# The first half of each pair's combination, with its loads, four turns sooner

## The chip, the core and the metric

The kernel runs on one core of a Trainium2 chip. The metric is the device time of one execution in microseconds (us). The core has five engines that work beside each other: PE (TensorE: matmuls and transposes), DVE (VectorE), ACT (ScalarE), POOL (GpSimd) and SP, which here only issues transfers (DMAs). Each engine does its own instructions in the order in which they are written into the program, and waits where an operand isn't ready. "PEld" in the profile is PE's loading of weights, which overlaps its matmuls.

## The reference

One layer of a decoder over 2048 tokens of width 1024, all in 32-bit floating point: a norm and one combined input projection, two mixers side by side, an output projection, a squared-ReLU MLP and a last norm. Mixer A is gated linear attention (GLA) in chunks, a recurrence over the tokens. Mixer B is dilated attention with 8 heads of 64 in three branches, which are then combined:

```
outs, lses = [], []
for window, dilation in ((128, 1), (512, 4), (2048, 16)):
    o, lse = dilated_branch(q, k, v, rel_bias, window, dilation)
    outs.append(o)
    lses.append(lse)
w = jax.nn.softmax(jnp.stack(lses, axis=0), axis=0)
return jnp.sum(w[..., None] * jnp.stack(outs, axis=0), axis=0)
...
mixed = jnp.concatenate([o_a, o_b], axis=-1)
h = h + jnp.einsum('bsm,md->bsd', mixed, w_out)
```

The last `sum` is the combination: for each token and head, the three branches' outputs are weighted by their softmax denominators and added.

## The kernel before

The program has stages one behind the other: the norm with the input projection (to about 522 us), the attention stage (to about 885 us), the output projection with the second norm, the MLP and the last norm. The change touches the attention stage alone.

**Turns.** The stage takes the 8 heads as four pairs (`pr` 0 to 3). Each head of a pair runs its branch 2 (dilation 16), then 1, then 0. A branch is cut into units of two or four blocks of 128 queries: 4 units for branch 2, 8 for branch 1, 8 for branch 0, so 40 units a pair and 160 in all. The main loop takes one turn for each unit. In a turn it writes, interleaved, the score matmuls of the unit three ahead (`AHEAD`; PE L764 and L766 into the PSUM banks `ps_c`, then DVE L776 adds the bias and takes the minimum, and ACT L777 the exponential, both in `pe`), the transposes of the present unit (PE L786 into `ps_d`, copied to `pt` by ACT L793 or DVE L795), and the products with the values of the unit two back (PE L805 into `ps_a`; DVE L808 copies the sums to the branch's output `O`). There are 384 score operations on DVE, two or four in a unit; places in the order are counted in them.

**GLA.** Beside the turns a generator gives one step of the GLA's 16 chunks at a time, 56 steps in 100 turns. A chunk is a chain over the engines: PE L932, ACT L933 and L934, POOL L935, L938 and L940, PE L945, DVE L946, PE L965 and L966, ACT L967 and L969, POOL L982, ACT L984, PE L990, DVE L993. All of PE's results in it go through one bank, `ps_o`. `gv` and `sr` are loaded by SP at L924 and L925. A chunk's 16 matmuls at L965 and L966 need its four at L945.

**The combination.** Branches 1 and 2 of a pair go to DRAM (`boD`) in their own order of tokens, and come back in the order of branch 0. While pair `pr` runs, pair `pr - 1` is combined, in two halves of 1024 tokens. Each half has two loads (SP L830, `cmb<-boD`) and eight steps, one a turn. Half 0 has its weights in the tile `small`; half 1 has them in a part of a GLA tile, which the profile names `gla`. The steps are: the minimum of the three logarithms' parts (DVE L842, L843) and its differences (POOL L845); the exponential (ACT L848) and the sum of the denominators (POOL L849 to L852); the reciprocal (DVE L855) and the weights (POOL L857); then, for each four tokens' tiles, the three multiplications and two additions (POOL L863 and L865). At the end a store of the combined tokens to `mixD` is noted, which SP issues three turns later (L882). Pair 3's own combination follows at the stage's end in four quarters and goes partly to DVE; the change leaves it alone.

**Other work on the same engines.** POOL also packs the queries for the dilated branches (L718, `qp<-qs`). In the last 28 turns `load_wo` brings in W_out in eight chunks: a load by SP (L1005, `woraw<-w_out`), a rounding on ACT (L1006) and the remainder on DVE (L1007).

**What sets the order.** The turns give what is written when. A scheduler then places each engine's instructions, by its own simulation of the times, so that one engine's instructions may stand in another order than the loop's. The minimum L842, the exponential L848 and the reciprocal L855 are held in program order (`tc.keep_in_program_order`). All tiles in SBUF called by `slot` share one ring of 25 places.

Of the kernel before, what the change touches and what calls it, by code (L numbers as in the profile page):

```python
# [38 lines left out]
def emit(tc, a, stop=99):  # L39
# [459 lines left out]
    def load_head(h):  # L499


        pr, hh = divmod(h, 2)
        t = pairs[h] = [slot("qs", FR, S)]
        pin(SP.dma_start(t[0].bitcast(F32), qD[pr][64 * hh:64 * hh + 64].rearrange("r d s -> (r d) s")), h)
        yield
        for part in range(2):
            t.append(slot(f"k{part + 1}", FR, S))
            rows = kD[pr][64 * hh:64 * hh + 64, part]
            pin(SP.dma_start(t[-1].bitcast(F32), bass.AP(tensor=rows.tensor, offset=rows.offset,
                                                         ap=[[2 * S, 64], [0, 2], [1, S]])), h)  # L510
            yield
# [313 lines left out]
    def combine_load(pr, half):  # L825

        ts, u = slice(8 * half, 8 * half + 8), slot("cmb")
        R = [view(u[:, 1056 * b:], (8, 132)) for b in range(2)]
        for b in range(2):
            SP.dma_start(R[b], boD[pr][b].rearrange("(t p) n -> p t n", p=128)[:, ts])  # L830
        return R
# [212 lines left out]
    def at_unit(n, *f):  # L1044
        plan.setdefault(n, []).append(f)
# [3 lines left out]
    def combine_at(pr, t0, n, at, steps):  # L1049

        if at is not None:
            at_unit(at + AHEAD, lambda: got.update({(pr, t0 // 8): combine_load(pr, t0 // 8)}))

        def step():
            if (pr, t0) not in running:
                running[pr, t0] = combine(pr, t0, n, got[pr, t0 // 8], V if pr == 3 and t0 % 8 else G)
            next(running[pr, t0], None)

        for k in steps:
            at_unit(k + AHEAD, step)  # L1060

    for pr in range(4):
        seq = [(hh, br) for hh in range(2) for br in (2, 1, 0)]
        if pr == 3:
            seq = [(0, 2), (0, 1), (1, 2), (1, 1), (0, 0), (1, 0)]
        for hh, br in seq:
            b = Branch()
            b.h, b.br = 2 * pr + hh, br
            m = 4 if br == 2 else 2
            first = len(units)  # L1070
            if br:
                for part in range(4) if first else ():
                    at_unit(first - 4 + part, pack_q, b.h, br, part)
            if br == 2 and first:
                pieces = load_head(b.h)
                for n in (13, 11, 8):
                    at_unit(first - n, lambda p: next(p), pieces)
                if hh == 0:
                    for half in range(2):
                        combine_at(pr - 1, 8 * half, 8, first - 2 + 7 * half, [first + 4 + 7 * half + n for n in range(8)])  # L1080
            if (pr, br) != (3, 0):
                for n in range(0, NT, m):
                    units.append(Unit(b, range(n, n + m)))
            elif hh:
                for n in range(0, NT, 4):
                    for w in (was, b):
                        units.extend(Unit(w, range(n + k, n + k + 2)) for k in (0, 2))
                for n, at in ((0, 8), (4, 11), (8, 14), (12, 18)):
                    combine_at(3, n, 4, first + 5 + n // 8 if n % 8 == 0 else None, [first + at + k for k in range(4)])
            was = b  # L1090
# [356 lines left out]
    first, parts_at = 7 * (NP - 1), {}  # L1447
# [3 lines left out]
    for at in range(7, len(jobs1)):  # L1451
# [13 lines left out]
        if at in (len(jobs1) - 4, len(jobs1) - 2):  # L1465
            n = (at + 4 - len(jobs1)) // 2
# [5 lines left out]
    for ph, (j, half) in enumerate(phases):  # L1472
        P = [bank() for _ in range(4)]
        for k in range(8):
            n = 8 * ph + k
# [53 lines left out]
def build(nc, inputs, stop=99):  # L1529
    arrays, aps = {}, {}  # L1530
    for name in _INS:
        arrays[name] = np.ascontiguousarray(inputs[name])
    arrays.update(_constants())
    for name, v in arrays.items():
        aps[name] = nc.dram_tensor(name, v.shape, mybir.dt.from_np(v.dtype), kind="ExternalInput").ap()
    aps["out"] = nc.dram_tensor("out", (1, S, D), F32, kind="ExternalOutput").ap()
    with tile.TileContext(nc, schedule_with_timeline_sim=True) as tc:
        emit(tc, aps, stop)
    return arrays
# [10 lines left out]
```

## Time and profile before

| | us |
|---|---|
| median of 3 runs (lowest, highest) | 2304.13 (2303.98, 2304.5) |
| profiled execution | 2305.64 |
| its span in the profile | 2303.9 |
| around the span | 1.74 |

A row of the timeline gives the start and the duration in us, the engine, the program line, the operation, what is written and what is read, and how many instructions lie in the row; in brackets stands the idle time ahead of it and what ended it. "SPq" is the part of SP that issues DMAs: such a row tells how long SP was at the issue, not how long the transfer took. In the groups by line the three numbers are the shortest, the median and the longest duration in ns. The granted clock of PE was 0.997 of full speed over the span.

### The profile page before, as it was taken

What the parts mean: (1) busy time and instruction counts of PE and PEld (TensorE: products, weight loads), DVE (VectorE), ACT (ScalarE), POOL (GpSimd) and SP (SyncE); (2) the same over time, 40 slices, a digit from 0 to 9 for tenths busy, and PEclk for the clock granted to TensorE, in tenths of its full rate; (3) what the DMA queues carried; (4) which work ended last, traced back from release to release, by engine and by line L of the source; (5) the groups of instructions that cost most, each with busy time, mean ns of one, the idle gap of its engine ahead of it and who ended that gap; (6) DMA issues with size and microseconds to landing.
All of it is one profiled execution on the core that took longest, in us unless ns stands there. A gap on an engine that the chain in (4) does not pass through costs nothing.

```text
span 2303.9 us, 34945 instructions
## 1 busy us (share of the span) xinstructions
PE 2281.4 (99%) x12700; PEld 1976.1 (86%) x12700; DVE 1533.8 (67%) x2846; ACT 1181.8 (51%) x2371; POOL 307.4 (13%) x394
## 2 busy tenths in 40 slices
PE   9999999999999999999999999999999999999998
PEld 8978998899999988888888888888888888888887
DVE  8787867756766675446777788777755446447444
ACT  6665536426877773335555566555544323225224
POOL 1210002024476671000000000000000100000002
PEclk9999999999999999999999999999999999999999
DMA  6467745776768764678544457444487477458543
GB/s 205 128 193 241 253 138 156 212 233 215 230 195 260 239 212 156 209 252 269 193 151 151 151 182 248 151 151 151 151 279 248 163 264 265 139 162 283 192 164 110
DMA packets 341805, 457.60 MB, mean 199 GB/s; under 512 B 18117, under 2 KB 214230, under 8 KB 336256
## 3 DMA queue, kind: packets, MB, share of 16 engines
q1 hardware_dynamic: 336878, 446.71, 59.8%
q10 hardware_dynamic: 4754, 8.66, 1.0%
q8 instruction: 100, 1.64, 0.3%
q14 instruction: 73, 0.60, 0.1%
HBM read 292.99 MB, written 167.02 MB: 200 GB/s over the span
## 4 chain that ended last, share of the span: by engine, by line
PE 95%; DMA 1%; POOL 1%; DVE 1%; ACT 1%; issue 1%; DVEq 0%; ACTq 0%; POOLq 0%; SPq 0%
PE ps_a L65 10%; PE ps_a L66 10%; PE ps_a L64 10%; PE ps_c L64 8%; PE ps_c L66 8%; PE ps_c L65 8%; PE ps_d L65 4%; PE ps_d L64 4%; PE ps_d L66 4%; PE ps_a L805 4%; PE ps_o L66 4%; PE ps_o L64 4%; PE ps_o L65 4%; PE ps_d L786 3%; PE ps_c L764 2%; PE ps_c L766 2%
## 5 line engine op out<-in xcount | busy, mean ns | idle before, releaser
L402 DVE TENSOR_TENSOR ca<-ra,ca 128x1024 fp32r<-128x1024 f32 x112 | 138.1, 1233 | 170.5 <-ACT ca L401 170.5
L401 ACT ACTIVATE ca<-ra 128x1024 fp32r<-128x1024 f32 x112 | 117.9, 1053 | 228.4 <-PE ps_c L66 189.8
L401 ACT ACTIVATE w1comb<-w1raw 128x512 fp32r<-128x512 f32 x224 | 140.0, 627 | 154.6 <-PE ps_c L66 54.5
L1377 POOL TENSOR_TENSOR suma<-suma,gs 128x512 f32<-128x512 f32 x16 | 23.4, 1477 | 1393.8 <-ACT scr L1375 1393.8
L402 DVE TENSOR_TENSOR w1comb<-w1raw,w1comb 128x512 fp32r<-128x512 f32 x224 | 154.0, 689 | 47.9 <-ACT w1comb L401 47.9
L805 PE MATMUL ps_a<-v,pt 128*128 128x65 f32 x1200 | 177.6, 252 | 3.1 <-ACT pt L793 1.7
L805 PEld LDWEIGHTS ps_a<-v,pt 128*128 128x128 f32 x1200 | 174.3, 194 | 4.4 <-ACT pt L793 2.0
L777 ACT ACTIVATE pe<-pe,O 128x256 f32<-128x256 f32 (+1 forms) x384 | 156.7, 453 | 40.1 <-DVE O L776 36.6
L786 PE MATMUL ps_d<-ident,pe 128*128 128x128 f32 x600 | 160.4, 280 | 0.0
L776 DVE CUSTOM_DVE_ANT_0 pe<-ps_c,nb 128x256 f32<-128x256 f32 (+1 forms) x384 | 126.8, 361 | 40.5 <-PE ps_d L786 19.1
L209 ACT ACTIVATE wcomb<-wraw 128x512 fp32r<-128x512 f32 (+2 forms) x119 | 90.1, 758 | 97.8 <-PE ps_a L65 28.4
L401 ACT ACTIVATE cb<-rb 128x1024 fp32r<-128x1024 f32 x56 | 59.4, 1061 | 151.6 <-PE ps_o L65 114.4
L66 PE MATMUL ps_c<-hb,w1comb 128*128 128x512 f32 x336 | 130.7, 389 | 0.0
L64 PE MATMUL ps_c<-hb,w1comb 128*128 128x512 f32 x336 | 130.7, 389 | 0.0
L65 PE MATMUL ps_c<-hb,w1comb 128*128 128x512 f32 x336 | 130.7, 389 | 0.0
L64 PE MATMUL ps_c<-cb,ca 128*128 128x512 f32 x336 | 130.7, 389 | 0.0
L65 PE MATMUL ps_c<-cb,ca 128*128 128x512 f32 x336 | 130.7, 389 | 0.0
L66 PE MATMUL ps_c<-cb,ca 128*128 128x512 f32 x336 | 130.7, 389 | 0.0
L402 DVE TENSOR_TENSOR cb<-rb,cb 128x1024 fp32r<-128x1024 f32 x56 | 68.3, 1222 | 64.3 <-ACT cb L401 64.3
L786 PEld LDWEIGHTS ps_d<-ident,pe 128*128 128x128 f32 x600 | 110.2, 188 | 0.1
L1239 ACT ACTIVATE acc<-acc 128x512 f32<-128x512 f32 x128 | 79.5, 631 | 51.0 <-DVE acc L1259 34.7
L64 PE MATMUL ps_a<-wo,mT 128*128 128x512 f32 x256 | 101.3, 396 | 0.0
(421 smaller groups left out, 7038.4 us busy)
## 6 DMA issues: line engine op xcount, KB each, us to landing
ra<-actD SPq DMA_DIRECT2D x56, 1024.0 KB, 6.7
actD<-acc SPq DMA_DIRECT2D x192, 256.0 KB, 2.5
rb<-w_ff SPq DMA_DIRECT2D x72, 512.0 KB, 4.8
w1raw<-w_ff SPq DMA_DIRECT2D x32, 1024.0 KB, 5.8
k<-kD SPq DMA_DIRECT2D x16, 1024.0 KB, 7.1
rb<-hTD SPq DMA_DIRECT2D x13, 1024.0 KB, 5.6
wraw<-w_in SPq DMA_DIRECT2D x48, 256.0 KB, 3.6
cmb<-boD SPq DMA_DIRECT2D x16, 528.0 KB, 7.1
```

Of the source, the lines that this page charges most:

```text
L64: T.matmul(out, sh, mh, start=first, stop=False)
L65: T.matmul(out, sl, mh, start=False, stop=False)
L66: T.matmul(out, sh, ml, start=False, stop=last)
L209: A.activation(hi, src, AF.Copy, scale=sc)
L401: A.activation(hi, src, AF.Copy)
L402: V.tensor_tensor(lo, src, hi.bitcast(F32), op=OP.subtract)
L764: T.matmul(s, q, k_cols(k1, br, first), start=True, stop=False)
L776: V.tensor_tensor_reduce(p, s, bias, scale=1.0, scalar=BIG, op0=OP.add, op1=OP.min, accum_out=nm)
L777: A.activation(p, p, AF.Exp, bias=nm, scale=-1.0)
L786: T.transpose(pb[:, i * 128:i * 128 + 128], src, ident)
L805: T.matmul(self.b.opsum[:, n % 4], self.pt[:, i * 128:i * 128 + 128], self.b.v[:, blk, cols], start=first, stop=last)
L1239: A.activation(v, v, AF.Relu)
```

## The change

For pairs 0 to 2, `first` is the turn at which the next pair's first unit stands, and `n` counts the eight steps of a half. Half 0's loads go from turn `first - 2` to `first - 6`, and its steps from `first + 4` to `first + 11` to `first` to `first + 7`. Half 1's loads stay at `first + 5` and its steps at `first + 11` to `first + 18`.

```diff
                 if hh == 0:
                     for half in range(2):
-                        combine_at(pr - 1, 8 * half, 8, first - 2 + 7 * half, [first + 4 + 7 * half + n for n in range(8)])
+                        combine_at(pr - 1, 8 * half, 8, first - 6 + 11 * half, [first + 11 * half + n for n in range(8)])
```

No instruction is added or removed; the scheduler places them anew. In the rows below, `O_7835` and `O_7840` are pair 2's branch 0 output, `O_8812` and `O_8817` pair 3's branch 1 output, before and after; `boD_0_102` and `boD_1_103` are pair 3's stored branches 1 and 2.

POOL at the end of pair 2's combination, before:

```order
L857 TENSOR_TENSOR gla<-gla 128x16 x3
L863 TENSOR_TENSOR O_7835<-O_7835,gla 128x4x128 x2
L863 TENSOR_TENSOR cmb<-cmb,gla 128x4x128 x4
L857 TENSOR_TENSOR small<-small 128x16 x3
L865 TENSOR_TENSOR O_7835<-O_7835,cmb 128x4x128 x2
L863 TENSOR_TENSOR O_7835<-O_7835,small 128x4x128 x2
L863 TENSOR_TENSOR cmb<-cmb,small 128x4x128 x4
L865 TENSOR_TENSOR O_7835<-O_7835,cmb 128x4x128
L938 TENSOR_TENSOR gla<-gla 64x2x128 x2
L940 TENSOR_TENSOR gla<-gla 128x2
L935 TENSOR_TENSOR gla<-gla 128x256
L865 TENSOR_TENSOR O_7835<-O_7835,cmb 128x4x128 x3
```

After, there are two places. Half 0 (`small`):

```order
L863 TENSOR_TENSOR O_7840<-O_7840,small 128x4x128 x2
L863 TENSOR_TENSOR cmb<-cmb,small 128x4x128 x4
L718 COPY qp<-qs 128x128x4 x4
L865 TENSOR_TENSOR O_7840<-O_7840,cmb 128x4x128 x2
L938 TENSOR_TENSOR gla<-gla 64x2x128 x2
L940 TENSOR_TENSOR gla<-gla 128x2
L935 TENSOR_TENSOR gla<-gla 128x256
```

and, ten rows further on, half 1 (`gla`):

```order
L857 TENSOR_TENSOR gla<-gla 128x16 x3
L863 TENSOR_TENSOR O_7840<-O_7840,gla 128x4x128 x2
L863 TENSOR_TENSOR cmb<-cmb,gla 128x4x128 x4
L865 TENSOR_TENSOR O_7840<-O_7840,cmb 128x4x128 x2
L938 TENSOR_TENSOR gla<-gla 64x2x128 x2
L940 TENSOR_TENSOR gla<-gla 128x2
L935 TENSOR_TENSOR gla<-gla 128x256
L865 TENSOR_TENSOR O_7840<-O_7840,cmb 128x4x128 x2
```

Before, the two halves stood back to back, with a GLA chunk's L938, L940 and L935 behind most of both. After, each half has one GLA chunk inside it, ahead of its last two additions.

DVE around pair 2's two reciprocals, before:

```order
L855 RECIPROCAL gla<-gla 128x16
L808 COPY O_8812<-ps_a 128x4x65
L776 ISA pe,O_8812<-ps_c,nb_5160 128x128
L776 ISA O_8812 128x1
L776 ISA pe,O_8812<-ps_c,nb_5160 128x128
L776 ISA O_8812 128x1
L795 COPY pt<-ps_d 128x512
L946 COPY_PREDICATED gla<-gla,ps_o 128x512
L855 RECIPROCAL small<-small 128x16
L776 ISA pe,O_8812<-ps_c,nb_5160 128x128
```

After, around the one of half 0:

```order
L776 ISA pe,O_8817<-ps_c,nb_5160 128x256
L776 ISA O_8817 128x1
L808 COPY O_8664<-ps_a 128x4x65
L855 RECIPROCAL small<-small 128x16
L776 ISA pe,O_8817<-ps_c,nb_5160 128x256
L776 ISA O_8817 128x1
```

and the one of half 1:

```order
L776 ISA pe,O_8817<-ps_c,nb_5160 128x256
L776 ISA O_8817 128x1
L776 ISA pe,O_8817<-ps_c,nb_5160 128x256
L776 ISA O_8817 128x1
L855 RECIPROCAL gla<-gla 128x16
L1007 TENSOR_TENSOR wo<-woraw,wo 128x1024
L993 TENSOR_TENSOR gla<-gla,ps_o 64x256 x2
```

Before, half 1's stood behind 336 of the 384 score operations L776 and half 0's behind 338, the later half first. After, half 0's stands behind 316 and half 1's behind 350. Half 0's minimum L842 went from behind 311 to behind 300. The same places of pair 1's half 0 are 215 and 220 before, 204 and 212 after.

SP around the store of pair 2's last half, before:

```order
L925 DMA gla<-srD 128x512
L1005 DMA woraw<-w_out 128x1024
L882 DMA boD_0_102<-O_8812 128x2x528
L882 DMA mixD<-gla 16x8x512
L882 DMA mixD<-O_7835 128x8x128
L924 DMA gla<-gvD 128x512
L830 DMA cmb<-boD_0_102 128x8x132
L830 DMA cmb<-boD_1_103 128x8x132
L830 DMA cmb<-boD_0_102 128x8x132
L830 DMA cmb<-boD_1_103 128x8x132
L1005 DMA woraw<-w_out 128x1024 x2
```

and after:

```order
L924 DMA gla<-gvD 128x512
L1005 DMA woraw<-w_out 128x1024
L882 DMA boD_0_102<-O_8817 128x2x528
L1005 DMA woraw<-w_out 128x1024 x2
L882 DMA mixD<-O_7840 128x8x128
L882 DMA boD_0_102<-O_8817 128x2x528
L830 DMA cmb<-boD_0_102 128x8x132
L830 DMA cmb<-boD_1_103 128x8x132 x2
L830 DMA cmb<-boD_0_102 128x8x132
L1005 DMA woraw<-w_out 128x1024
L882 DMA mixD<-gla 16x8x512
L1005 DMA woraw<-w_out 128x1024
```

The gv load (L924) and two loads of W_out went from behind the store `mixD<-O_...` to ahead of it, and one store of pair 3's branch 1 from ahead to behind. On PE, the GLA's last L965 and L966 stood behind all 384 scores and now stand behind 376; the last two L945 stood behind 358 and 382 and now stand behind 348 and 368. All of PE's instructions are the same ones, and their order up to about 616 us and in the later stages is unchanged.

## The prediction

> **What bounds the kernel now.** I read the page first, then the stretches of time, then PE's waits in the attention stage, and last the timelines of POOL, SP, DVE and ACT around those waits.
>
> ```profile
> span 2303.9 us, 34945 instructions
> PE 2281.4 (99%) x12700; PEld 1976.1 (86%) x12700; DVE 1533.8 (67%) x2846; ACT 1181.8 (51%) x2371; POOL 307.4 (13%) x394
> ```
> PE is busy 2281.4 of 2303.9 us, so a reordering can win no more than PE's idle time in the stage that it touches. It can lose as much as it makes PE wait.
>
> ```profile
> 535.00:616.00 81.00, 81.00 (x731) 80.17 (x731) 55.60 (x240) 61.09 (x176) 30.46 (x40) 1.00 0.60 193
> 616.00:820.00 204.00, 204.00 (x1834) 201.85 (x1833) 143.59 (x619) 160.42 (x484) 138.99 (x208) 1.00 0.75 235
> 820.00:850.00 30.00, 26.17 (x236) 25.33 (x235) 23.25 (x75) 23.48 (x61) 23.18 (x22) 1.00 0.71 224
> 850.00:880.00 30.00, 27.39 (x216) 25.79 (x215) 25.12 (x72) 20.64 (x61) 18.96 (x34) 0.94 0.70 222
> ```
> Each row is a stretch of the attention stage: its start and end, its length, PE's busy time, then PEld, DVE, ACT, POOL, the granted clock and the DMA share. PE has no idle time from 535 to 820, which holds the combinations of pairs 0 and 1 and most of that of pair 2. Its idle time is 30.00 - 26.17 = 3.83 us from 820 to 850 and 30.00 - 27.39 = 2.61 us from 850 to 880, 6.44 us together.
>
> ```profile
> PE ps_o L945 <- POOL gla L935: 2.1, 1, 2.1
> PE ps_a L805 <- ACT pt L793: 1.7, 1, 1.7
> PE ps_a L805 <- DVE pt L795: 1.4, 2, 0.9
> PE ps_o L965 <- ACT gla L934: 1.2, 1, 1.2
> ```
> These are all of PE's waits from 535 to 890: 2.1 + 1.7 + 1.4 + 1.2 = 6.4 us. Only the first has POOL behind it, the engine on which the moved steps run.
>
> ```profile
> 810.14 0.58 POOL L857 TENSOR_TENSOR gla<-gla 128x16 f32<-128x16 f32 x3 [0.36 <-DVE gla L855]
> 810.68 2.05 POOL L863 TENSOR_TENSOR O<-O,gla 128x512 f32<-128x512 f32 x2
> 812.69 5.03 POOL L863 TENSOR_TENSOR cmb<-cmb,gla 128x512 f32<-128x512 f32 x4
> 817.68 0.58 POOL L857 TENSOR_TENSOR small<-small 128x16 f32<-128x16 f32 x3
> 818.22 2.54 POOL L865 TENSOR_TENSOR O<-O,cmb 128x512 f32<-128x512 f32 x2
> 820.72 2.05 POOL L863 TENSOR_TENSOR O<-O,small 128x512 f32<-128x512 f32 x2
> 822.72 5.04 POOL L863 TENSOR_TENSOR cmb<-cmb,small 128x512 f32<-128x512 f32 x4
> 827.72 1.29 POOL L865 TENSOR_TENSOR O<-O,cmb 128x512 f32<-128x512 f32 x1
> 828.96 2.43 POOL L938 TENSOR_TENSOR gla<-gla 64x256 f32<-64x256 f32 x2
> 831.62 0.73 POOL L935 TENSOR_TENSOR gla<-gla 128x256 f32<-128x256 f32 x1
> 832.30 4.83 POOL L865 TENSOR_TENSOR O<-O,cmb 128x512 f32<-128x512 f32 x3
> 838.31 2.54 POOL L865 TENSOR_TENSOR O<-O,cmb 128x512 f32<-128x512 f32 x2
> ```
> This is POOL (start, duration). Both halves of pair 2's combination stand back to back, with the GLA's L938 and L935 behind: that is PE's 2.1 us. POOL is through at 838.31 + 2.54 = 840.85.
>
> ```profile
> 840.87 0.56 SPq L882 DMA_DIRECT2D mixD<-O  x1
> 841.53 2.15 SPq L924 DMA_DIRECT2D gla<-gvD  x1
> 843.78 7.53 SPq L830 DMA_DIRECT2D cmb<-boD  x4
> 851.36 2.46 SPq L1005 DMA_DIRECT2D woraw<-w_out  x2
> ```
> SP issues in order. The store of pair 2's combined output stands until POOL is done, and behind it come the gv load, pair 3's four combination loads and the last two loads of W_out.
>
> ```profile
> 858.04 1.06 ACT L1006 ACTIVATE wo<-woraw 128x1024 fp32r<-128x1024 f32 x1 [1.80 <-DMA woraw<-w_out]
> ```
> ACT then stands 1.80 us for the seventh W_out chunk, with the last exponentials and pt copies behind it. PE's later waits hang on this one release.
>
> **The change, part by part.** It adds and removes nothing; for pairs 0 to 2 it moves half 0's two loads and eight steps four turns ahead.
>
> *Loads.* Six DMAs move past other entries of SP's queue.
>
> ```profile
> cmb<-boD SPq DMA_DIRECT2D x16, 528.0 KB, 7.1
> ```
> Each lands 7.1 us after issue in the median. Loads and steps move together, so the distance between them stays. What SP issues behind them (gv, qs, v and k of the next pair) can be late by two issues, which by the 7.53 us for four is 2 x 1.88 = 3.8 us; nothing from 535 to 820 made PE wait, so 0 there, with 3.8 us as the upper end.
>
> *Pairs 0 and 1.* Half 0's POOL work is, by its rows, 0.58 + 2.05 + 5.04 + four adds of 1.27 = 12.7 us. The 345 us of the four stretches hold nearly all of the stage's 160 turns, some 2 us each, so it now starts about 8 us sooner, with the same neighbours on POOL.
>
> ```profile
> 613.93 1.44 POOL L938 TENSOR_TENSOR gla<-gla 64x256 f32<-64x256 f32 x2 [11.16 <-ACT gla L933]
> ```
> Just ahead of pair 0's steps POOL stood idle for 11.16 us: there is room. Cost 0; PE covers it. If the block delays a GLA L935, PE pays what exceeds the GLA's slack, at most 2.1 us each as in the tail, twice: 4.2 us as the upper end, which the 204.00 busy of 204.00 makes unlikely. GLA steps also come about one step earlier in PE's order, which changes no duration.
>
> *Pair 2, half 0.* Its block leaves the tail, so that one half stands behind the GLA there. The 2.1 us at 830 go. That alone is no gain at the end, since PE would then wait longer for ACT's release at 858.04; the gain is what moves that release and what PE finds to do before it.
>
> *Pair 2, half 1.* Its reciprocal L855 stood behind the 336th score operation on DVE; it now stands behind the 350th.
>
> ```profile
> 821.76 0.42 DVE L776 CUSTOM_DVE_ANT_0 pe<-ps_c,nb 128x256 f32<-128x256 f32 x1
> 822.49 1.35 DVE L1007 TENSOR_TENSOR wo<-woraw,wo 128x1024 fp32r<-128x1024 f32 x1 [0.31 <-ACT wo L1006]
> ```
> The 350th ran at 821.76, ahead of this L1007. On PE the GLA runs a step ahead in the new order, so four more L945 and sixteen more L965/L966 stand ahead of that score.
>
> ```profile
> 832.40 1.13 PE ps_o L945 x4
> 869.26 0.39 PE L965 MATMUL ps_o<-gla 128*128 128x128 f32 x2
> 870.82 0.39 PE L966 MATMUL ps_o<-gla 128*128 128x128 f32 x2
> ```
> The four take 1.13 us (a row of the chain). The other two are the first and last of eight rows, the sixteen matmuls of the GLA's last step, which ended at 871.05: 1.8 us. The reciprocal then comes at 821.76 + 0.42 + 1.13 + 1.8, about 825. From there POOL has 0.58 + 2.05 + 5.03 + 2.54, then L938 2.43, L940 and L935 0.93, then two adds 2.54: 16.1 us, so it ends at 841, with 841.5 for handovers, against 840.85. The half that moved away does not make POOL finish sooner, because the other half now starts later. Bounds: 839.5 to 843.
>
> *SP's tail.* gv (2.15) and two W_out chunks stand ahead of the store now, no longer behind it; one boD store (0.4) comes behind it. The seventh chunk's issue moves by +0.65 - 2.15 + 0.4 = -1.1 us. I take the release 1.1 us sooner; bounds, by POOL's end, 3.1 sooner to 0.4 later.
>
> *The GLA's last step.* Its sixteen matmuls at 869.26 (1.8 us) stood behind all 384 scores and now stand behind 376, where PE would be waiting for ACT: 1.8 us less at the end. Against it I set 0.4 us, since the last L945 now comes within about a microsecond of POOL's L935 (bounds 0 to 2.1).
>
> *A rule on ports.* The nearest rows to DVE working beside POOL's block:
>
> ```profile
> L1007 DVE TENSOR_TENSOR wo<-woraw,wo x8: 1215/1235/1945, 813.9 to 865.0; 128x1024 fp32r<-128x1024 f32 x8
> ```
> The one at 822.49, begun inside POOL's multiplications, took 1.35 us against a median of 1.235 (minimum, median, maximum in ns): 0.1 us. The Trainium skill ("SBUF — State Buffer", section "🔬 SBUF: two separate sides") says that a VectorE operation with two SBUF inputs and a GpSimd operation that reads SBUF lock each other out for the whole instruction. By it, three L1007 beside half 1's block would each wait for up to one multiplication, 5.03 / 4 = 1.26 us, or 3.8 us in all, which gives 2305.4 us. No such hold shows at 822.49, so the sum goes by the rows.
>
> *Sum.* 0 + 0 - 1.1 - 1.8 + 0.4 = -2.5 us. The profiled execution took 2305.64 us (its span 2303.9 and 1.74 around it), so it would be 2303.1; the median of the runs, 2304.13, lies 1.5 lower, and 2.5 off it gives 2301.6.
>
> **Rivals.** *A: all the tail's idle time goes.* If POOL's end comes early in its bounds, the release comes 3 us sooner and the 1.7 and 1.4 us waits go too: all 6.4 us, 2297.7. For it: every wait there descends from POOL's back-to-back block. Against: the reciprocal's new place.
>
> *B: slower, by a hold on DVE.* DVE keeps its written order. Half 0's minimum (L842) in pair 2 now stands behind 300 score operations and its reciprocal behind 316, where before the reciprocal stood behind 338 and never waited.
>
> ```profile
> 779.93 0.29 DVE L776 CUSTOM_DVE_ANT_0 pe<-ps_c,nb 128x128 f32<-128x128 f32 x1
> 791.25 0.16 DVE L843 TENSOR_TENSOR small<-small,cmb 128x16 f32<-128x16 f32 x1
> 794.05 0.42 DVE L776 CUSTOM_DVE_ANT_0 pe<-ps_c,nb 128x256 f32<-128x256 f32 x1 [0.21 <-PE ps_c L766]
> 794.89 4.00 POOL L718 CAST qp<-qs 128x512 fp32r<-128x512 f32 x4 [2.83 <-PE ps_c L766]
> 804.65 0.22 POOL L852 TENSOR_TENSOR small<-small 128x16 f32<-128x16 f32 x1
> ```
> The 300th and the 317th score ran at 779.93 and 794.05: 14.1 us of room. POOL's path between them, L843 to the last L852, took 804.87 - 791.25 = 13.6 us, with the query copy inside it (4.00, and 2.83 of waiting). Above 14.1 us of path DVE waits, with the scores' L776, the O copies L808 and PE's transposes queued behind; above about 16.6 the kernel is slower than before. One more wait of that copy (2.83 + 4.00) and one L982 (1.3) give 13.6 + 8.1 = 21.7, a hold of 7.6 us: 2309.2. Against it: some of the 13.6 was other work that now lies elsewhere. The same can befall pair 1, which has the same shape.
>
> *C: the change does nothing at the end.* Release and last step stay tied to pair 3's four loads: 2304 us.
>
> **Numbers.** The forecast has 0.36, A 0.28, B 0.30, C 0.06. A measurement of this kernel tells about 0.2%, 4.6 us. A is faster by more (0.28), and the forecast's lower edge adds 0.03: 0.31. B is slower by more for 0.26 and the shorter holds, 0.04, are within; with the forecast's 0.33 and C's 0.06 that makes 0.43. The forecast's own range is 2299.5 (release at its best, -4.5) to 2304.8 (release 0.4 later, the hold 2.1). The whole range goes down to 2296.5, a little under A, since the idle time is read from busy records and not from the runs, and up to 2309.5, B with its hold; it leaves out longer or repeated holds and deeper gains.
>
> **What would show it.** Right: no PE idle from 535 to 820; DVE's L855 of half 0 without idle ahead of it; half 1's block on POOL from about 825 to 841; no PE wait at L945 above 1 us; the seventh W_out load issued near 850 and ACT's L1006 near 857; the last L965/L966 before that. Wrong: idle time on DVE ahead of L855 released by POOL L852, PE waiting for ACT's pe or pt in pairs 1 or 2, a combination load that makes L842 wait, or POOL done with pair 2 clearly before 839.

## The result: 0.13% slower

Over 22 runs each, the changed kernel took 2307.16 us in the median (2304.9 to 2310.15) and the kernel before 2304.78 (2301.62 to 2307.36). The ratio is 1.0013, with a 95% interval of 1.0007 to 1.0019, that is 3.0 us more (1.6 to 4.4); the two medians lie 2.4 us apart. The forecast was 2301.6 with a range of 2296.5 to 2309.5: the time lies in the range, on the wrong side of before.

The page of the changed kernel:

```profile
span 2308.0 us, 34940 instructions
PE 2283.3 (99%) x12700; PEld 1977.4 (86%) x12700; DVE 1538.0 (67%) x2846; ACT 1181.4 (51%) x2371; POOL 307.2 (13%) x394
```

The stretches of time that held PE's idle time before, after the change (columns as in the prediction's table):

```profile
820.00:850.00 30.00, 28.58 (x252) 27.55 (x251) 27.17 (x85) 25.12 (x66) 20.08 (x24) 1.00 0.69 224
850.00:880.00 30.00, 25.58 (x212) 24.29 (x212) 23.28 (x76) 18.47 (x50) 13.98 (x30) 0.94 0.77 240
```

PE's idle time went from 3.83 to 1.42 us in the first and from 2.61 to 4.42 us in the second. Its waits from 535 to 895 us are now these:

```profile
PE ps_a L805 <- ACT pt L793: 3.4, 2, 2.8
PE ps_a L805 <- DVE pt L795: 2.5, 3, 1.2
```

POOL's L935 no longer holds PE (2.1 us before); ACT's `pt` does, for 2.8 us at once. Behind the attention stage stand two more waits, at the start of the MLP, which the prediction left out. First in the kernel before, in the execution that the prediction reads, then in the changed one:

```profile
PE ps_d L65 <- DVE w1comb L402: 0.6, 1, 0.6
PE ps_d L64 <- ACT hb L401: 0.5, 1, 0.5
```

```profile
PE ps_d L64 <- ACT hb L401: 1.4, 1, 1.4
PE ps_d L65 <- DVE w1comb L402: 1.3, 1, 1.3
```

To compare executions by stage, I count from a place that all of them reach without idle time after it until 820: the first L945 of the GLA's fourth chunk (604.86 us in the trace of before, 606.11 in that of the changed kernel, 602.64 and 604.96 in the second traces; these differences arose where the two programs are still the same). The starts of some PE instructions after it, in us; "again" is a second trace of the same program, from the experiments:

| | before | before, again | changed | changed, again |
|---|---|---|---|---|
| last product with values (L805) | 272.55 | 273.15 | 272.91 | 273.01 |
| in the output projection (near 953 us) | 348.08 | 348.71 | 348.90 | 349.00 |
| behind the MLP's first wait (near 1107) | 501.89 | 501.55 | 503.66 | 503.63 |
| behind its second wait (near 1448) | 842.65 | 842.35 | 845.53 | 845.86 |
| PE's last matmul | 1691.06 | 1691.11 | 1693.94 | 1694.27 |

The mean of the changed kernel's two traces less that of before's two is +0.1 us at the end of attention, +0.55 in the output projection, +1.9 behind the MLP's first wait and +3.2 behind the second, +3.0 at the end. So by these marks the attention stage gave neither gain nor loss, though PE's clock has a part in that (last section), and most of the loss appears in stages whose instructions the change left alone.

In the attention stage itself the predicted gain is missing. These are POOL, SP, ACT, DVE and PE in the changed kernel's tail, in that order, each from its timeline:

```profile
827.24 1.43 POOL L857 TENSOR_TENSOR gla<-gla 128x16 f32<-128x16 f32 x3 [3.81 <-DVE gla L855]
835.63 2.52 POOL L865 TENSOR_TENSOR O<-O,cmb 128x512 f32<-128x512 f32 x2
838.12 2.42 POOL L938 TENSOR_TENSOR gla<-gla 64x256 f32<-64x256 f32 x2
841.46 3.51 POOL L865 TENSOR_TENSOR O<-O,cmb 128x512 f32<-128x512 f32 x2
```

```profile
844.99 0.38 SPq L882 DMA_DIRECT2D mixD<-O  x1
...
846.05 6.03 SPq L830 DMA_DIRECT2D cmb<-boD  x4
852.18 1.68 SPq L1005 DMA_DIRECT2D woraw<-w_out  x1
```

```profile
860.28 1.06 ACT L1006 ACTIVATE wo<-woraw 128x1024 fp32r<-128x1024 f32 x1 [3.66 <-issue]
```

```profile
841.82 2.01 DVE L1007 TENSOR_TENSOR wo<-woraw,wo 128x1024 fp32r<-128x1024 f32 x1 [0.28 <-ACT wo L1006]
...
861.37 1.23 DVE L1007 TENSOR_TENSOR wo<-woraw,wo 128x1024 fp32r<-128x1024 f32 x1 [6.08 <-ACT wo L1006]
```

```profile
862.16 0.44 PE L805 MATMUL ps_a<-v,pt 128*128 128x65 f32 x2 [2.77 <-ACT pt L793]
```

Take 1.25 us off each to compare with before. The reciprocal ended POOL's wait at 825.99, about where it was expected (825). But POOL ended at 843.72, not 841.5 (before 840.85), the store left SP at 843.74, the seventh W_out chunk was asked for at 850.93 (before 851.36) and rounded at 859.03 (before 858.04): 1.0 us later than before, where 1.1 sooner was forecast. Its transfer took 8.1 us from issue to use, against 6.7 before. Before's second trace, set on the same anchor, has 849.95 and 857.05 there, so against it the changed kernel asked 1.0 us later and rounded 2.0 later. Ahead of the rounding ACT stood 3.66 us and DVE, which takes the remainder after ACT's rounding, 6.08 us, with `pt` copies and scores queued behind on both; PE stood with them. In before, DVE stood 1.52 us at the same chunk:

```profile
859.13 1.50 DVE L1007 TENSOR_TENSOR wo<-woraw,wo 128x1024 fp32r<-128x1024 f32 x1 [1.52 <-DMA mx<-mixD]
```

### The profile page after: what moved, and what is told of

Its sections match the earlier page's. It is cut to its first block, busy times and chain, and to the rows that moved or that the text cites. A ratio compares the mean times of both kernels' runs of the same rounds, so it can differ in the third digit from the quotient of the medians.

```text
span 2308.0 us, 34940 instructions
## 1 busy us (share of the span) xinstructions
PE 2283.3 (99%) x12700; PEld 1977.4 (86%) x12700; DVE 1538.0 (67%) x2846; ACT 1181.4 (51%) x2371; POOL 307.2 (13%) x394
## 4 chain that ended last, share of the span: by engine, by line
PE 50%; DVE 1%; DMA 1%; ACT 1%; issue 0%; ACTq 0%; DVEq 0%
PE ps_c L64 6%; PE ps_c L66 6%; PE ps_c L65 6%; PE ps_a L66 4%; PE ps_a L65 4%; PE ps_d L64 4%; PE ps_a L64 4%; PE ps_d L65 4%; PE ps_d L66 4%; PE ps_o L64 2%; PE ps_o L66 2%; PE ps_o L65 2%; DMA rb<-hTD 0%; DMA hTD<-tb 0%; DVE hb L402 0%; DVE w1comb L402 0%
## 5 line engine op out<-in xcount | busy, mean ns | idle before, releaser
L805 PE MATMUL ps_a<-v,pt 128*128 128x65 f32 x1200 | 179.0, 252 | 5.8 <-ACT pt L793 3.4
L805 PEld LDWEIGHTS ps_a<-v,pt 128*128 128x128 f32 x1200 | 174.9, 194 | 8.1 <-ACT pt L793 3.8
L776 DVE CUSTOM_DVE_ANT_0 pe<-ps_c,nb 128x256 f32<-128x256 f32 (+1 forms) x384 | 126.4, 360 | 40.3 <-PE ps_d L786 18.7
```

Of the source, the lines that this page charges most:

```text
L776: V.tensor_tensor_reduce(p, s, bias, scale=1.0, scalar=BIG, op0=OP.add, op1=OP.min, accum_out=nm)
L805: T.matmul(self.b.opsum[:, n % 4], self.pt[:, i * 128:i * 128 + 128], self.b.v[:, blk, cols], start=first, stop=last)
```

## The experiments

Each was timed over the same rounds as the kernel before, on the same chip. A ratio is to before's runs there, with its 95% interval; "marks" are the five of the table above. In kernels with a longer source the line numbers behind the edit are one to five higher. A difference given in us is the ratio's, applied to before's time.

### The changed kernel once more, and before once more

No edit.

> The changed kernel once more, for a second trace of it. Theory T (tail): the time is lost because half 1 of pair 2 is finished on POOL later than before (its reciprocal behind 350 scores, POOL held beside DVE's L1007), so that the store of pair 2 and the last W_out and first out-projection loads leave SP later: slower than before by 2 to 4 us, the last L865 of pair 2 again 2 to 3 us later than before, counted from the stage's first score. Rival R (chance): most of the difference sits in the waits at the start of the MLP (near 1105 and 1395 us), which one execution has and the next has not: then this trace shows those waits at the size of before (0.6 and 0.5 us) and the median stays within 1.5 us of before.

Measured: 2306.57 us, 1.0013 (1.0004 to 1.0021).

> The kernel before, for a second trace. If the changed kernel's later losses (0.4 us in the out projection, 1.0 and 1.1 to 1.6 us at the two waits of the MLP) belong to the change, this trace has those waits at 0.5 to 0.7 us again; if they come and go with the execution, one of them is at 1.3 us or more here. The half-speed episodes of PE's clock (two of 3.4 us in before, none with pair 2 alone) show whether they repeat.

Measured: 2303.86 us, 0.9999 (0.9989 to 1.0009). The later waits, first of the changed kernel, then of before:

```profile
PE ps_d L64 <- ACT hb L401: 1.4, 1, 1.4
PE ps_d L65 <- DVE w1comb L402: 1.0, 1, 1.0
PE ps_c L65 <- DVE w1comb L402: 0.4, 2, 0.2
```

```profile
PE ps_d L64 <- ACT hb L401: 0.5, 1, 0.5
```

The changed kernel repeats its waits, before repeats the smaller one and lacks the other. So rival R (chance) falls, by the ratio above all; that these waits belong to the program rather than to the execution rests on two traces of each. Theory T had POOL's end right (2.9 us later than before in both traces), though not yet that it was the cause.

### Pair 2 alone, and pairs 0 and 1 alone

```diff
-                        combine_at(pr - 1, 8 * half, 8, first - 2 + 7 * half, [first + 4 + 7 * half + n for n in range(8)])
+                        early = 4 if pr == 3 and half == 0 else 0
+                        combine_at(pr - 1, 8 * half, 8, first - 2 - early + 7 * half, [first + 4 - early + 7 * half + n for n in range(8)])
```

For pairs 0 and 1 the condition is `pr < 3` (the loop's `pr` is one more than the pair combined).

> Only pair 2's half 0 goes four turns sooner; pairs 0 and 1 stay as before. The reciprocal of pair 2's half 1 stands behind 348 scores, of half 0 behind 306. Theory T: as the whole change, 2 to 4 us above before, since only pair 2's tail counts. Rival M (middle): pairs 0 and 1 cost something of their own, and this one is within 1 us of before.

Measured: 2302.22 us, 0.9990 (0.9981 to 0.9999): 2.3 us faster than before, where theory T expected a loss. POOL and ACT in the tail:

```profile
835.35 3.50 POOL L865 TENSOR_TENSOR O<-O,cmb 128x512 f32<-128x512 f32 x2
```

```profile
854.13 1.06 ACT L1006 ACTIVATE wo<-woraw 128x1024 fp32r<-128x1024 f32 x1 [1.99 <-DMA woraw<-w_out]
```

Against the anchor (603.77) POOL ends at 235.1, before 236.0; the seventh chunk is rounded at 250.4, before 253.2 and 252.2; the last L805 comes at 269.91, before 272.55 and 273.15. So the chunk and the end of the stage both come sooner, by 1.8 to 2.8 and 2.6 to 3.2 us. In part it is PE's clock: this trace has no stretch at half speed in the tail, and both of before's have (last section); whether the new order keeps it away is not shown. The granted clock of a run was 0.999 or more in 10 of 11 runs here and in 6 of before's 33. Among the runs at 0.999, pair 2 alone took 2302.4 us in the mean and before 2303.4, 1 us apart.

> Half 0 of pairs 0 and 1 alone four turns sooner; pair 2 as before. In this order the GLA runs a step ahead from pair 1 on, as in the changed kernel (its last L945 behind 362 of 384 scores; before 382, pair 2 alone 380, changed kernel 368). Theory G (GLA ahead): PE does a GLA step more before the 348 scores behind which DVE's reciprocal of pair 2's half 1 stands, so that reciprocal, POOL's last additions, the store and the seventh W_out chunk come later, and PE lacks that step while it waits: 1 to 4 us slower than before, ACT's seventh W_out rounding 335 to 338 us after the first score (335.4 before, 331.2 with pair 2 alone). Rival P (pair 2 is needed too): within 1 us of before.

Measured: 2303.07 us, 0.9998 (0.9989 to 1.0007): no change that can be told, so theory G missed, and no cost of pairs 0 and 1 by themselves is seen. The trace shows more than the time does. Its last L805 comes at 269.98, 2.6 to 3.2 us sooner than before, although the seventh chunk is rounded at 255.1, 1.9 to 2.9 later than before. The gain is gone behind the MLP's first wait (503.59, before 501.55 and 501.89). This execution took 2306.19 us, 3.1 above the median of its runs, and PE's clock was low just there (a mean of 0.91 from 1095 to 1115 us), so what it loses in the MLP need not be the program's. Some of its waits:

```profile
PE ps_c L426 <- DMA mx<-mixD: 2.1, 1, 2.1
PE ps_d L65 <- DVE w1comb L402: 2.0, 1, 2.0
```

The two parts do not add up: -2.3 and about -0.5 us alone, +3.0 together. What differs among these orders in the tail is where the work on the seventh W_out chunk stands. On DVE its remainder (L1007) stands behind 380 of the 384 score operations before, 379 with pair 2 alone, 382 with pairs 0 and 1 alone and 376 in the changed kernel; on ACT its rounding stands behind 378, 376, 378 and 376 exponentials. This suggests that with 382 and 378 a chunk that lands late holds little, and that with pair 2 alone it holds much but lands early; the changed kernel has the early place and the late landing. The hold further down tests it.

### The GLA a step ahead with pair 2 alone

```diff
-G0, GE = 8, 56
+G0, GE = 6, 56
```

on top of pair 2 alone.

> Pair 2 alone moved, pairs 0 and 1 as before, but the GLA begins at turn 6, not 8. In this order its last L945 stands behind 364 scores, not 380; the reciprocal of half 1 stays behind 348. Theory G: the gain of pair 2 alone (2.3 us under before) turns into a loss, 0 to 4 us above before, POOL's last addition of pair 2 at least 2 us later than with pair 2 alone. Rival M (pairs 0 and 1 cost something of their own, whatever the GLA does): it stays 1 to 4 us faster than before.

Measured: 2304.14 us, 1.0000 (0.9991 to 1.0009). The gain of pair 2 alone does not show, and it is no loss: the ratio lies at the edge of theory G's band (0 to 4 us above before) and outside rival M's, and its interval of 2.1 us either way reaches into both. Counted from the stage's first score, POOL ends 321.3 us in, against 316.0 with pair 2 alone, as G said. So POOL can end much later, and the GLA can run ahead, without the changed kernel's loss.

### Half 1 eight turns sooner as well

```diff
-                        combine_at(pr - 1, 8 * half, 8, first - 6 + 11 * half, [first + 11 * half + n for n in range(8)])
+                        combine_at(pr - 1, 8 * half, 8, first - 6 + 3 * half, [first + 3 * half + n for n in range(8)])
```

The new line is written here in the form of the change's own.

> As the changed kernel, and half 1's loads and steps also eight turns sooner for pairs 0 to 2. In this order the reciprocal of pair 2's half 1 stands behind 336 scores, as before, with half 0's next to it, and POOL's last additions of pair 2 come earlier. Theory T: the loss goes and half of the predicted gain comes: between 3 us faster and 1 us slower than before. Rival R or M: as slow as the changed kernel, 2 to 4 us above before.

Measured: 2308.46 us, 1.0020 (1.0011 to 1.0029): as slow as the changed kernel, or slower. With the reciprocal back behind 336 scores, the loss did not go, so the reciprocal's place does not carry it. POOL's last addition, though, still ended at 239.3 from the anchor (changed kernel 238.9, before 236.0), not sooner as was expected. So this run does not yet speak against theory T's other half, that POOL's late end carries the loss; the two runs that follow bear on that.

### The subtraction on DVE taken away

```diff
-            V.tensor_tensor(w[:, 1], raw, w[:, 0].bitcast(F32), op=OP.subtract)
+            V.memset(w[:, 1].bitcast(F32), 0.0)
```

on the changed kernel.

> The changed kernel with DVE's L1007 (W_out's remainder, two inputs from SBUF) replaced by a fill with zeros, which reads nothing; W_out's low part is left out of the output. If the port lock of DVE and POOL is what stretched POOL's L857 (1.43 for three instead of 0.58) and last two L865 (3.51 instead of 2.54), both return to 0.6 and 2.5 us, POOL is through 1.8 us sooner, and the kernel is 1 to 2 us faster than the changed one. If the lock is not the cause, the rows stay stretched and the time is the changed kernel's within 1 us.

Measured: 2306.77 us, 1.0008 (0.9999 to 1.0017). The rows of L857 on POOL for the `gla` half, first of the changed kernel, then of this one (shortest, median and longest in ns):

```profile
L857 POOL TENSOR_TENSOR gla<-gla x12: 201/222/1074, 652.4 to 878.2; 128x16 f32<-128x16 f32 x9, 128x8 f32<-128x8 f32 x3
```

```profile
L857 POOL TENSOR_TENSOR gla<-gla x12: 202/222/223, 649.8 to 875.8; 128x16 f32<-128x16 f32 x9, 128x8 f32<-128x8 f32 x3
```

The stretched one, 1074 ns, is gone; in the changed kernel it ran beside a L1007 of DVE's that had begun just ahead of it (827.08 and 827.24 us). The end of POOL's block comes at 236.2 from the anchor (238.9 in the changed kernel) and the seventh chunk at 252.5 (254.2). Both are back where before has them (236.0; 253.2 and 252.2). The kernel is nevertheless not faster than the changed one beyond the interval (the difference of 1.2 us would fit the expectation, but the intervals overlap): other waits came (1.3 us for ACT's `mT`, 1.2 us for POOL's L865). On ACT the seventh chunk's rounding stands behind 374 exponentials; on DVE its fill stands behind 368 scores, and the eighth chunk's, behind 376, stood 2.27 us until that rounding was done. That a shorter block on POOL and an earlier chunk take the loss away is not shown.

### The reciprocal on POOL

```diff
-        tc.keep_in_program_order(V.reciprocal(Z[:, 1], Z[:, 0]))
+        G.tensor_tensor(Z[:, 1], Z[:, 0], view(gst["minus"], (n, 2)), op=OP.pow) if pr < 3 else tc.keep_in_program_order(V.reciprocal(Z[:, 1], Z[:, 0]))
```

with a tile `gst["minus"]` filled with -1.

> The changed kernel with the reciprocal of pairs 0 to 2 on POOL (a power of -1) in place of DVE, so that no half waits for its turn among DVE's scores; price of the power unknown, taken as under 1 us. The order that comes of it has the GLA not ahead (last L945 behind 375), and pair 3's four loads and the last but two W_out loads ahead of pair 2's last store. Theory G with the pinned reciprocal as the carrier: POOL is through with pair 2 at 318 us after the first score or sooner (changed kernel 321.1), the seventh W_out chunk at 333 or sooner, 1 to 5 us faster than before. Rival: the tail is bound by the transfers themselves (pair 3's four loads of 528 KB and W_out), then the seventh chunk comes at 335 to 336 again and the time is within 1 us of before.

> Pair 2 alone moved, with the reciprocal on POOL as in the run reciprocal_on_pool; here the order has the GLA ahead (last L945 behind 360). If the GLA's place acts only through the pinned reciprocal, this is as fast as reciprocal_on_pool, 1 to 5 us under before. If PE misses the GLA's step in the tail whatever the reciprocal does, it is slower than reciprocal_on_pool by 2 us or more.

Measured: 2309.52 us, 1.0019 (1.0010 to 1.0028), and 2303.48 us, 0.9996 (0.9987 to 1.0004). The price was misjudged:

```profile
833.07 2.91 POOL L855 TENSOR_TENSOR gla<-gla 128x16 f32<-128x16 f32 x1
```

A power on POOL takes 2.91 us where DVE's reciprocal takes 0.25, and POOL ended later in both (248.4 and 248.2 from the anchor), not sooner. The second is 6 us faster than the first, which neither side expected. These two say nothing on the pinned reciprocal, but the second has POOL's end 12 us later than before and no loss: a late end on POOL alone does not make it.

### The last two W_out roundings held back

On the changed kernel; the loads stay where they are.

```diff
-            A.activation(w[:, 0], raw, AF.Copy)
-            V.tensor_tensor(w[:, 1], raw, w[:, 0].bitcast(F32), op=OP.subtract)
             WO.append(w)
+
+            def fin(raw=raw, w=w, c=c):
+                r = A.activation(w[:, 0], raw, AF.Copy)
+                c > 5 and tc.keep_in_program_order(r)
+                V.tensor_tensor(w[:, 1], raw, w[:, 0].bitcast(F32), op=OP.subtract)
+
+            at_unit(NU - 28 + 3 * c + AHEAD + 4, fin) if c > 5 else fin()
```

> The changed kernel with the rounding of the last two W_out chunks on ACT (L1006) held behind the exponentials of 382 and 384 scores; in the changed kernel they stand behind 376 and 381 (in pairs01_only behind 382 and 384, before behind 380 and 384). Loads, POOL and everything ahead of the last twenty scores keep their order. Theory W: PE starves in the tail because the seventh chunk lands late (336 us after the first score) and ACT stands at it with exponentials and pt copies behind; with it behind 382 scores PE's wait of 2.8 us for ACT's pt goes, the last L805 comes at 351 to 353 us after the first score (changed kernel 355.1), and the time is 2 to 4 us under the changed kernel's, that is from 2 us faster than before to 1 us slower. Rival D (downstream): the attention stage ends sooner, but the waits at the start of the MLP (1.3 and 1.4 us) grow by as much, within 1 us of the changed kernel.

Measured: 2303.37 us, 0.9995 (0.9986 to 1.0004), 3.2 to 3.8 us under the changed kernel's two medians; its interval ends where theirs begins. Its marks are 272.74, 348.72, 501.55, 842.36 and 1690.99: those of before's second trace within 0.5 us each. (The counts in the expectation are DVE's; on ACT the two roundings went from behind 376 and 376 exponentials to behind 378 and 383.) The stalls at the chunk and the MLP's longer waits are gone; ACT and DVE at the seventh chunk, and PE's waits from 535 to 1420 us:

```profile
856.49 1.06 ACT L1009 ACTIVATE wo<-woraw 128x1024 fp32r<-128x1024 f32 x1 [0.28 <-issue]
```

```profile
858.22 2.13 DVE L1011 TENSOR_TENSOR wo<-woraw,wo 128x1024 fp32r<-128x1024 f32 x1
```

```profile
PE ps_a L805 <- DVE pt L795: 2.7, 2, 1.6
PE ps_a L805 <- ACT pt L793: 1.6, 2, 1.2
PE ps_d L64 <- ACT hb L401: 0.5, 1, 0.5
```

The chunk is rounded no sooner (254.1 from the anchor, 254.2 in the changed kernel), and POOL, in the same order, ends at the same 238.9. What differs stands from 247 to 290 us after the anchor, on ACT, DVE and PE, and on SP, where the eighth chunk's load goes out 2.0 us sooner and the output projection's first `mx` loads some 4 us later. Against before the loss is gone, the part in the MLP too. Rival D, by which the MLP's waits grow, falls.

Theory W has the time right and the wait of 2.8 us, but not the way. From the anchor the stage ends at 272.74, against 272.91 and 273.01: PE waits 4.3 us in the tail and no longer 5.9, but its clock is at half speed there for 6.8 us and not 3.4, which costs 1.7 us more. (From the first score the last L805 comes at 352.9, in the band, only because this execution lost 2.1 us less ahead of the anchor.) What holding the roundings gains appears behind the stage.

The same hold, with `+ 6`, which puts both remainders behind 384 scores, on before and on pair 2 alone:

> The kernel before with the same hold (both last W_out roundings behind 384 scores; before 380 and 384), none of the combinations moved. Theory W: PE's 1.7 us wait for ACT's pt near 862 us goes, 1 to 4 us faster than before. Rival: the chunk is waited for later, by the out projection, and the time stays within 1 us of before.

> Pair 2 alone moved, with the hold (384 and 384; pair2_only 379 and 381). Theory W: its waits of 0.7 and 1.0 us in the tail go, 2299 to 2302 us, the fastest so far. Rival: at the size of pair2_only (2302.2) or slower, since the seventh chunk already lands at 331 us there and the out projection waits for it then.

Measured: 2302.16 us, 0.9993 (0.9984 to 1.0002), and 2303.52 us, 0.9996 (0.9987 to 1.0004). The first may be a gain of 1.6 us, which its interval doesn't settle; in its trace the last L805 comes at 266.41, over 6 us sooner than before, and PE's last matmul only 3.1 sooner. With the hold in both, the changed kernel stands at 0.9995 and before at 0.9993, with medians 1.2 us apart. So the hold may help any of these orders, and a part of the change's loss may be left under it; the runs don't settle either. The second misses its band, as the rival had it: with a chunk that lands early, holding it back buys nothing, and the eighth chunk's rounding moves to 263.7 from the anchor, against 253.1 with pair 2 alone. Of all kernels tried, pair 2 alone is the one whose interval excludes no change on the faster side, by 0.0001, which among so many is little.

The place and the landing over all orders that take the remainder on DVE (the chunk's rounding on ACT in us from the anchor):

| | scores ahead of the seventh remainder | chunk rounded | ratio to before |
|---|---|---|---|
| changed | 376 | 254.2, 254.3 | 1.0013, 1.0013 |
| half 1 eight turns sooner as well | 378 | 255.3 | 1.0020 |
| pair 2 alone | 379 | 250.4 | 0.9990 |
| before | 380 | 253.2, 252.2 | 1, 0.9999 |
| reciprocal on POOL | 380 | 258.4 | 1.0019 |
| pair 2 alone, reciprocal on POOL | 381 | 255.3 | 0.9996 |
| pairs 0 and 1 alone | 382 | 255.1 | 0.9998 |
| pair 2 alone, GLA a step ahead | 382 | 257.7 | 1.0000 |
| changed, held | 382 | 254.2 | 0.9995 |
| before, held | 384 | 254.6 | 0.9993 |
| pair 2 alone, held | 384 | 254.0 | 0.9996 |

From 381 on, none of these orders is slower than before beyond its interval, with chunks as late as 257.7; below that, the three orders with a chunk later than before's are slower and the one with an earlier chunk is not. The orders differ in other things too, so this goes with the hold's result and does not prove it.

## Why the prediction was wrong, step by step

**Pairs 0 and 1, and the loads, at nothing:** right. No idle time stands on PE from 535 to 820, and pairs 0 and 1 alone measure 0.9998.

**Rival B, DVE held at half 0's reciprocal:** did not come. The changed kernel's idle time on DVE ahead of all its reciprocals that waited for POOL:

```profile
  POOL small L852: 0.4, 1
```

That is 0.4 us, once. POOL waited for DVE instead. **Rival A, all the tail's idle time gone:** did not come either; 5.84 us of idle time stand where 6.44 stood.

**Pair 2's half 0:** right in that the wait for L935 (2.1 us) went. Pair 2 alone measures 2.3 us, close to the sum's 2.5, but that is luck: the GLA's term of 1.8 us is not in it, since there the GLA's last L965 still stands behind all 384 scores, and a part of the gain goes with the clock.

**The reciprocal of half 1 at about 825:** right within 1 us (825.99 by the clock of before). **POOL's end at 841.5:** mis-sized, 843.72, beyond the stated bound of 843. Three L857 took 1.43 us and not 0.58, the last two L865 3.51 and not 2.54, beside DVE's L1007, one of which took 2.01 us itself. With the start 1.0 us later that is about the 2.6 us by which POOL ended behind the rows' sum of 841.1. This is the rule on ports that was weighed and set aside, and the reading that set it aside was wrong. At 822.49 it was not DVE that was kept waiting, with its 1.35 us, but POOL: one of the four multiplications from 822.72 on took 2.03 us, the other three 1.05. The row of 5.04 us has that wait inside. First before, from 803 to 842 us, then the whole run without the subtraction:

```profile
L863 POOL TENSOR_TENSOR cmb<-cmb,small x4: 1046/1048/2027, 822.7 to 826.7; 128x512 f32<-128x512 f32 x4
```

```profile
L863 POOL TENSOR_TENSOR cmb<-cmb,small x14: 1043/1047/1052, 618.6 to 866.8; 128x512 f32<-128x512 f32 x14
```

Each of the four L1007 beside POOL's block in before (813.86, 822.49, 828.85 and 832.27) has one POOL instruction at about 1 us over its like. The sum took two such waits over with the rows of 5.03 and 2.43 us; the changed kernel has four in half 1's block alone. By the Trainium skill ("SBUF — State Buffer", section "🔬 SBUF: two separate sides") a VectorE operation with two SBUF inputs and a GpSimd operation that reads SBUF shut each other out; the trace agrees with the 1074 ns against 222, and the run without the subtraction with the 223 ns. One engine's row without a wait says nothing of the other's.

**SP's tail, -1.1 us:** this step failed. The chunk was issued 0.4 us sooner than in before's first trace and 1.0 later than in its second, not 1.1 sooner; from issue to use it took 1.0 to 1.5 us longer, and its rounding came 1.0 to 2.1 us later.

**The GLA's last step, -1.8 us:** this step failed too, and it weighs most. It took for granted that the same work as before waits behind the chunk. In the new order the seventh chunk's remainder stands behind 376 scores on DVE, before behind 380, and the late chunk holds the scores and `pt` copies that PE needs. PE's waits for L945 and L965, 3.3 us, did go, but those for `pt` grew from 3.1 to 5.9 us. That place stood in the order on DVE and ACT; the prediction did not ask there what stands behind the chunk. Holding those two chunks' work back to behind 382 and 384 scores takes the loss against before away, with the reserve that the same hold may speed up the kernel before by 1.6 us.

**The stages behind, at nothing, unsaid:** wrong. They hold 2.9 of the 3.0 us. That the waits for `w1comb` and `hb` belong to the tail's order is likely, since they come in both traces of the changed kernel and not in the one with the hold. How it comes about is not shown. The instructions there are in the same order in all these kernels, and up to about 460 us after the anchor SP issues 0.8 to 0.9 us later than in before's first trace in the changed kernel and 0.6 later in before's second and with the hold; 20 us on it is 1.9 and 2.0 against 0.1 and 0.4. A later arrival is not the rule either: pairs 0 and 1 alone come there 2.2 us sooner and lose 1.7 of it. It stays open.

**The bound, PE's idle time in the stage:** too narrow. The prediction's row from 850 to 880 has a granted clock of 0.94; the half-speed stretch of 3.4 us in it costs 1.7 us that count there as busy. (A slip: 2304.13 - 4.5 is 2299.6, not 2299.5.)

## What to carry to other kernels

When a moved block changes when a late transfer lands, look on every engine at what stands behind the instruction that waits for it, after the change as well as before: here a few scores' difference went with 3.2 to 3.8 us between medians, more than the 2.5 that the block's move was to gain. Where a scheduler places such an instruction by its own idea of the landing, and the transfer lands late, try to hold it behind the work that doesn't need it. And a part that measures as a gain alone can be a loss beside another that measures as nothing: try them apart before the sum is believed. And where two engines may lock each other out, read the longest duration on both: a row of four instructions hides the one that waited.

## What was not expected of the hardware

PE's clock was granted at half speed for short stretches after waits in the tail. In before, from 865.1 to 868.5 us, the granted clock is 0.50. The windows from 860 to 870 us of before, of its second trace, and of pair 2 alone (the clock is third from the end):

```profile
860.00:870.00 10.00, 7.39 (x53) 6.88 (x52) 9.89 (x28) 7.27 (x17) 4.21 (x4) 0.83 0.76 236
```

```profile
860.00:870.00 10.00, 8.72 (x58) 8.53 (x57) 9.52 (x32) 5.37 (x13) 3.32 (x7) 0.66 0.89 299
```

```profile
860.00:870.00 10.00, 8.27 (x76) 7.87 (x76) 9.90 (x30) 8.06 (x26) 8.96 (x14) 1.00 0.50 178
```

A mean of 0.83 over 10 us is 3.4 us at half speed, 1.7 us of PE's work; 0.66 is 6.8 us and 3.4 us of work. Before's second trace has one more, of 3.4 us from 830.5, so 10.2 us in the tail against 3.4 in its first; the two end within 0.1 us of each other. The changed kernel has 3.4 us in both traces. So part of what a shorter wait gives is taken or given by where such a stretch falls. What sets one off is not settled here: in before the wait just ahead of it was 1.7 us, and the wait of 2.1 us at 832 had none behind it, while the same wait, 2.0 us, in the second trace had one. The Trainium skill ("TensorE: Matmul & The Clock Gate", section "What's actually happening") gives a free-running window of 3413 ns, which agrees with the 3.4 and 6.8 us here.
